# Two Winograd pairs per feed-forward column group, with the weight sums prepared in HBM by accumulating transfers

## The chip, the cores and the metric

The kernel runs on one core of one Trainium2 chip. A time is the device time of one execution in microseconds (us); the number to compare is the median over runs. A core has five engines with instruction queues of their own: TensorE (PE, matrix products), VectorE (DVE), ScalarE (ACT), GpSimd (POOL) and SyncE (SP). SP and POOL issue most of this kernel's DMA transfers. Each queue is worked off in order, so an instruction that waits holds back everything behind it on the same queue.

## The reference, cut to what matters

One decoder layer on 256 tokens of width 2048, all in float32: an input projection, two kinds of token mixers, an output projection, a gated feed-forward layer with a causal width-3 convolution, and a last gated addition. The change concerns the feed-forward layer:

```python
h = rms_norm(x, ffn_norm_g[i])
u = h @ w_up[i]                       # (256, 2048) @ (2048, 2 * 5632)
a, g = jnp.split(u, 2, axis=-1)       # two halves of 5632 columns
a = causal_dwconv(a, conv_w[i], conv_b[i])
x = x + (jax.nn.gelu(a, approximate=False) * g) @ w_down[i]
```

## The kernel before, in words

**Products.** Every weight block that PE uses is first split into two float32r parts, `hi` (a cast on ACT) and `lo` (raw minus `hi`, on DVE). A product of a 128 x 128 block of activations (kept as hi and lo too) with a 128 x 512 block of weights is then three matmuls: hi·hi, hi·lo and lo·hi. The function `three` (line 1291) issues them for the up projection.

**The stages.** First stretch: input projection, mixers and output projection run as 153 weight blocks of up to 512 KB, streamed by `run_stream` with three raw buffers, three blocks split ahead of PE. Then the feed-forward layer and the last gate run as a list of units handled by `run_units`: a unit has a load (SP), a split (ACT and DVE, four pairs of `hi`/`lo` buffers) and a function that issues matmuls. The up projection is 11 column groups `q` of 4 x 128 columns of `a` and the matching 512 columns of `g`. Tokens come in two halves t = 0, 1 and the columns in two halves n = 0 (`a`) and n = 1 (`g`), so a group has four PSUM banks. A plain unit takes one chunk `k` of 128 inputs: 4 products, 12 matmuls.

**The seven.** In groups 1 to 10 the chunks k = 0 and 1 are not plain. With the chunks and token halves as a 2 x 2 block matrix on the left, and chunks and column halves as one on the right, Winograd's scheme makes the same result with seven products in place of eight: 21 matmuls for 24. Three products (P5, P6, P7) use sums of left blocks `S_up` (made once by `up_sums`), and sums of right blocks, that is, of weights. The kernel before makes these weight sums on DVE in every group: `seven` loads four blocks into `xs` (line 1314 to 1316), three subtractions (lines 1323 to 1325) make T1, T2 and T4, and four units split and multiply. P1, P5, P6, P7 go to four banks of their own; lines 1355 to 1361 combine them into `z_up` (in `xs`), scaled, which is added to the group's rows later.

**The end of a group.** `up_rows` (ACT, line 887) scales the four banks into `EZ`; `up_turn` adds `z_up` (DVE, line 894), transposes 32 x 32 blocks into `Y` (DVE, line 184) and `move` (line 186) issues 16 DMA transfers from `Y` back to `EZ`, all on POOL. In the next group the jobs of `up_act` follow, spread over units: `first` copies the `a` half into `Y` (ACT, line 901), four `conv` jobs make the convolution into `c_`, the second half of `Y` (ACT line 906, DVE line 909), and `last` does GELU, the product with `g`, and the split (lines 915, 916, 140, 141). The left sums of the down projection go to HBM (`sums<-Sp`, POOL).

**What sets the order.** Python code issues the instructions; a scheduler of the framework then places them on each queue by its own estimate of times. `tc.issue_after(...)` keeps an instruction behind a given one. Raw buffers in the up projection are the three of `raw` and five spare ones (`v0` to `v4`); `free_raws` says which unit may use which.

Of the kernel before, what the change touches and what calls it, by code (L numbers as in the profile page):

```python
# [9 lines left out]
F32 = mybir.dt.float32  # L10
# [35 lines left out]
LOAD_AT, SUMS_AT, SEVEN_AT = 5, 2, 6  # L46
# [3 lines left out]
def layer_kernel(  # L50
# [135 lines left out]
    def move(y, c):  # L186

        for a in range(4):
            for b in range(4):
                pool.dma_start(out=c[32 * b : 32 * b + 32, a::4], in_=y[32 * a : 32 * a + 32, :, b])  # L190
# [54 lines left out]
    def run_stream(blocks, pulls, ramp=False):  # L245
# [4 lines left out]
        for i in range(-AHEAD_DMA, nb):  # L250
            j = i + AHEAD_DMA
            if j < nb:
# [5 lines left out]
                nc.sync.dma_start(out=raws[j][:, : kb * n].rearrange("p (k n) -> p k n", k=kb), in_=src)  # L258

# [17 lines left out]
            if i >= 0:  # L277
                blocks[i][1](*parts.pop(i))
                done[0] += 1
                pull(pulls)  # L280

# [3 lines left out]
    def token_group(w, korder, actT, c0, n, finish, tag="mm", prep=None, load=None):  # L285
# [26 lines left out]
        return blocks  # L312

# [29 lines left out]
    with mixers:  # L343
# [462 lines left out]
        run_stream(blocks, 2, ramp=True)  # L806
# [3 lines left out]
    with tc.tile_pool(name="ffn", bufs=1) as fp:  # L810
# [6 lines left out]
        S_up = fp.tile([P, 4, 256], F32R, tag="u42", name="S_up")  # L817
        spares = {"u32": (4, 2), "u36": (4, 2), "u40": (2, 1)}
        spare_raws = {k: fp.tile([P, n // 2, BLK], F32, tag=k, name=f"{k}r") for k, (n, _) in spares.items()}
# [26 lines left out]
        B_up = xs[:, 0]  # L846
# [11 lines left out]
        def sums_of(u, f, t):  # L858

            (a11, a21), (a12, a22) = ((u[:, j, 0:P], u[:, j, P:S]) for j in range(2))  # L860
            dve.tensor_add(f[:, 0], a21, a22)
            dve.tensor_sub(f[:, 1], f[:, 0], a11)
            dve.tensor_sub(f[:, 2], a11, a21)
            dve.tensor_sub(f[:, 3], a12, f[:, 1])
# [12 lines left out]
        c_ = Y[:, BLK : 2 * BLK].rearrange("p (k s) -> p k s", k=4)  # L877
# [11 lines left out]
        def up_turn(q):  # L889
# [6 lines left out]
            move(y, Z)  # L896

        def up_act(q):

# [32 lines left out]
        def free_raws(j):  # L932

            def may(t):
                if t[0] == "v":
                    return 7 <= j < 16 + 18 * until[t]
# [4 lines left out]
        def new_raw(j, name):  # L941
# [7 lines left out]
            if tag[0] == "v":  # L949
                i = int(tag[1])  # L950
                return spare_raws[f"u{32 + 4 * (i // 2)}"][:, i % 2]
# [48 lines left out]
        def part(hi, lo, raw):  # L1000
            act.copy(hi, raw)  # L1001
            last["hi"] = traced()
            dve.tensor_sub(lo, raw, f32(hi))  # L1003
# [30 lines left out]
        def down(c0, X_tag, P_tag, sums_done, done, at, pairs, sevens):  # L1034
# [39 lines left out]
            def seven(p_, hook):  # L1074
# [24 lines left out]
                def split3(hi, lo):  # L1099
                    ra, rb_ = first.raws  # L1100
                    dve.tensor_sub(half(ra, 0), half(ra, 1), half(ra, 0))
                    dve.tensor_sub(half(ra, 1), half(rb_, 1), half(ra, 1))  # L1102
# [6 lines left out]
                def split4(hi, lo):  # L1109
                    ra, rb_ = first.raws  # L1110
                    dve.tensor_sub(half(rb_, 1), half(rb_, 1), half(ra, 0))
                    dve.tensor_sub(half(rb_, 0), half(rb_, 0), half(rb_, 1))
# [28 lines left out]
        def sums_done(c0):  # L1141

            def f(b):
                both = xs[:, 1, c0 : c0 + 1024].rearrange("p (n c) -> p n c", n=2)
                x00, x01 = (xs[:, 0, c0 + n * 512 : c0 + (n + 1) * 512] for n in range(2))
                right = xs[:, :, c0 + 512 : c0 + 1024]

                def twice(v):
# [310 lines left out]
```

## Time and profile before

| | us |
|---|---|
| median of 3 runs | 1241.52 |
| lowest and highest run | 1240.97, 1242.49 |
| the profiled execution, its own time | 1241.07 |
| its span in the profile | 1239.1 |

The span is the time from the first to the last recorded instruction. Of the up projection, group 0 begins near 444 us and group 10 ends near 918 us; the down projection and the gate follow. The busy time of an engine is not by itself a cost: what counts is where PE waits. "Landing" is the time from a transfer's issue to its completion.

### The profile page before, as it was taken

The page shows a single profiled execution, that of the slowest core. Times are in us where ns is not written, and L with a number is a line of the kernel's source. Part 1 is how long each engine was busy: PE and PEld are TensorE (multiplying, and loading weights), DVE is VectorE, ACT ScalarE, POOL GpSimd, SP SyncE. Part 2 cuts the span into 40 slices and gives each one's busy share as a digit, 9 for nine tenths or more (in the row PEclk, how much of TensorE's full clock was granted, in tenths as well). Part 3 has the DMA queues.
Part 4 walks back from the last instruction along what each step waited for, and adds up shares of the span by engine and source line. Part 5 has one row for each costly group of instructions (what it writes and reads, how often), then busy time and mean ns, then how long its engine had stood idle before and what let it go on. Part 6 is the DMA issues. An engine that isn't in the chain of part 4 may idle for free.

```text
span 1239.1 us, 16191 instructions
## 1 busy us (share of the span) xinstructions
PE 1232.5 (99%) x5638; PEld 1039.3 (84%) x5638; DVE 901.0 (73%) x1125; ACT 720.9 (58%) x1000; POOL 244.2 (20%) x457
## 2 busy tenths in 40 slices
PE   9999999999999999999999999999999999999998
PEld 7999988888888888888888888888888888888887
DVE  5455566665565665888888898888778998998653
ACT  7565455554554454766676576657645555566542
POOL 2001256513304202022202211220220000050000
PEclk9999999999999999999999999999999999999999
DMA  8766877766557797776877777676895996777560
GB/s 242 207 187 185 233 215 220 207 194 177 173 187 223 217 340 219 223 227 217 260 236 212 224 254 243 192 237 193 257 294 171 316 359 204 264 236 251 179 211 34
DMA packets 134370, 276.35 MB, mean 223 GB/s; under 512 B 15065, under 2 KB 30033, under 8 KB 134161
## 3 DMA queue, kind: packets, MB, share of 16 engines
q1 hardware_dynamic: 118864, 249.66, 64.3%
q0 software_dynamic: 15040, 25.50, 7.2%
q8 instruction: 44, 0.72, 0.2%
q14 instruction: 37, 0.30, 0.1%
q10 hardware_dynamic: 385, 0.16, 0.0%
HBM read 247.46 MB, written 8.93 MB: 207 GB/s over the span
## 4 chain that ended last, share of the span: by engine, by line
PE 99%; DMA 0%; SPq 0%; DVE 0%; ACT 0%; issue 0%; DVEq 0%
PE tg L304 13%; PE tg L305 13%; PE tg L306 13%; PE up L1292 12%; PE up L1294 12%; PE up L1293 12%; PE dnP L1054 1%; PE dnP L1055 1%; PE dnP L1053 1%; PE upP L1292 1%; PE upP L1294 1%; PE upP L1293 1%; PE dn(0, 1)_7885 L1055 1%; PE dn(0, 0)_7881 L1054 1%; PE dn(0, 1)_7885 L1054 1%; PE dn(1, 0)_7889 L1054 1%
## 5 line engine op out<-in xcount | busy, mean ns | idle before, releaser
L275 DVE TENSOR_TENSOR lo<-raw,hi 128x1024 fp32r<-128x1024 f32 (+3 forms) x153 | 177.7, 1162 | 154.8 <-ACT hi L273 154.4
L1294 PE MATMUL up<-hi,x2T 128*128 128x512 f32 x644 | 250.7, 389 | 0.0
L1293 PE MATMUL up<-lo,x2T 128*128 128x512 f32 x644 | 250.6, 389 | 0.0
L273 ACT CAST hi<-raw 128x1024 fp32r<-128x1024 f32 (+3 forms) x153 | 153.1, 1001 | 155.3 <-PE tg L306 122.7
L1292 PE MATMUL up<-hi,x2T 128*128 128x512 f32 x644 | 221.3, 389 | 0.0
L305 PE MATMUL tg<-lo,hT 128*128 128x512 f32 (+2 forms) x480 | 181.5, 379 | 0.0
L304 PE MATMUL tg<-hi,hT 128*128 128x512 f32 (+2 forms) x480 | 180.9, 382 | 0.0
L306 PE MATMUL tg<-hi,hT 128*128 128x512 f32 (+2 forms) x480 | 180.3, 377 | 0.0
L1003 DVE TENSOR_TENSOR lo<-raw,hi 128x1024 fp32r<-128x1024 f32 (+1 forms) x118 | 137.2, 1171 | 43.4 <-ACT hi L1001 42.8
L1001 ACT CAST hi<-raw 128x1024 fp32r<-128x1024 f32 (+1 forms) x118 | 118.8, 1014 | 81.6 <-PE up L1294 35.9
L1294 PEld LDWEIGHTS up<-hi,x2T 128*128 128x128 f32 x644 | 120.9, 188 | 25.1
L1293 PEld LDWEIGHTS up<-lo,x2T 128*128 128x128 f32 x644 | 120.9, 188 | 25.0
L1292 PEld LDWEIGHTS up<-hi,x2T 128*128 128x128 f32 x644 | 120.9, 188 | 25.0
L190 POOL DMA_DIRECT2D EZ<-Y x176 | 93.1, 536 | 122.7 <-DVE Y L184 52.1
L306 PEld LDWEIGHTS tg<-hi,hT 128*128 128x128 f32 x480 | 90.1, 188 | 12.5
L305 PEld LDWEIGHTS tg<-lo,hT 128*128 128x128 f32 x480 | 90.2, 188 | 11.7 <-DVE lo L275 0.3
L304 PEld LDWEIGHTS tg<-hi,hT 128*128 128x128 f32 x480 | 89.7, 188 | 11.7
L1001 ACT CAST hi<-xs 128x1024 fp32r<-128x1024 f32 (+1 forms) x43 | 40.8, 952 | 71.1 <-PE up L1294 50.0
L1003 DVE TENSOR_TENSOR lo<-xs,hi 128x1024 fp32r<-128x1024 f32 (+1 forms) x43 | 47.1, 1098 | 34.7 <-ACT hi L1001 34.7
L873 POOL DMA_DIRECT2D sums<-Sp x9 | 5.2, 575 | 272.3 <-DVE Sp L866 272.3
L1003 DVE TENSOR_TENSOR lo<-u36r,hi 128x1024 fp32r<-128x1024 f32 x36 | 43.6, 1215 | 11.8 <-ACT hi L1001 10.3
L1001 ACT CAST w<-raw 128x1024 fp32r<-128x1024 f32 x27 | 28.4, 1053 | 38.3 <-DVE raw L1102 27.1
(695 smaller groups left out, 2351.9 us busy)
## 6 DMA issues: line engine op xcount, KB each, us to landing
raw<-in_w_in_dram SPq DMA_DIRECT2D x71, 512.0 KB, 4.2
raw<-in_w_up_dram SPq DMA_DIRECT2D x68, 512.0 KB, 5.2
raw<-in_w_down_dram SPq DMA_DIRECT2D x43, 512.0 KB, 6.0
u36r<-in_w_up_dram SPq DMA_DIRECT2D x36, 512.0 KB, 5.0
raw<-in_w_in_dram SPq DMA_DIRECT2D x40, 432.0 KB, 3.8
raw<-in_w_out_dram SPq DMA_DIRECT2D x32, 512.0 KB, 4.7
u32r<-in_w_up_dram SPq DMA_DIRECT2D x31, 512.0 KB, 5.2
EZ<-Y POOLq DMA_DIRECT2D x176, 64.0 KB, 4.6
```

Source lines behind the costliest of these rows:

```text
L190: pool.dma_start(out=c[32 * b : 32 * b + 32, a::4], in_=y[32 * a : 32 * a + 32, :, b])
L273: act.copy(hi, raw[:, :w])
L275: dve.tensor_sub(lo, raw[:, :w], f32(hi))
L304: pe.matmul(o, ah, hi[:, i, :], start=first, stop=False)
L305: pe.matmul(o, ah, lo[:, i, :], start=False, stop=False)
L306: pe.matmul(o, al, hi[:, i, :], start=False, stop=last)
L1001: act.copy(hi, raw)
L1003: dve.tensor_sub(lo, raw, f32(hi))
L1054: pe.matmul(o, ah, lo, start=False, stop=False)
L1292: pe.matmul(o, ah, hi, start=start, stop=False)
L1293: pe.matmul(o, ah, lo, start=False, stop=False)
L1294: pe.matmul(o, al, hi, start=False, stop=stop)
```

## The change

**Two sevens per group.** In groups 1 to 10 the chunks k = 0 to 3 are taken by two sevens (`SEVENS_UP` = 2); 12 plain units are left instead of 14. P1, P5, P6 and P7 of the two are summed in the same four banks, so that the combination of line 1355 to 1361 is still made once. A group has 20 units: four plain, the first seven's four, three plain, the second seven's four, five plain (`FIRST_AT`, `SECOND_AT`).

**The weight sums come from HBM.** `up_jobs` makes for each of the 20 sevens a DRAM tile `upT` of four 128 x 512 slots: a plain transfer on SP copies a block into two slots, accumulating transfers on POOL add blocks to them (two in the first job), a second SP transfer copies slot 0 to slots 2 and 3, and three more accumulating transfers add to these. Signs in `sums_of`, `sums_done` and the down projection's splits are turned so that only additions are needed. Twelve of the 20 sets are made during the first stretch (from block 18 on, every 11 blocks, the second job 12 blocks after the first), the other eight during groups 0 to 5 (from unit 12 on, every 14 units, the second job 7 units later). A seven's units then load like weights: 512 KB, 512 KB, 512 KB and 256 KB. The subtractions of lines 1323 to 1325 and the `B_up` loads are gone.

**Conv results in memory of their own.** `c_` is now in `xs` (except in the last group), not in `Y`; the spare raw buffer `v4` is in `xs` too. The jobs of `up_act` sit at units 9, 10, 11, 12, 15 and 16 of a group's 20 (before: 10 to 15 of 18). `move` puts every other transfer on SP, eight on each queue. The `lo` subtraction that follows an `up_turn` is kept behind it.

POOL's queue before, at the end of the first stretch and the first up groups (`x2z` is the residual's transposed rows, `EZ<-Y` the moves of a group's end, `sums<-Sp` the left sums):

```order
L190 DMA x2z<-x2y 32x2x128 x48
L165 TENSOR_TENSOR rstd_ffn<-rs_v,neghalf 128x2
L190 DMA EZ<-Y 32x2x256 x32
L873 DMA sums<-Sp 128x1024
L190 DMA EZ<-Y 32x2x256 x16
```

and the same place now (L332 is an accumulating transfer; the moves are L193):

```order
L168 TENSOR_TENSOR rstd_ffn<-rs_v,neghalf 128x2
L332 DMA upT_1_158<-in_w_up_dram 128x512
L332 DMA upT_0_159<-in_w_up_dram 128x512 x2
L193 DMA EZ<-Y 32x2x256 x8
L332 DMA upT_0_159<-in_w_up_dram 128x512 x3
L332 DMA upT_1_160<-in_w_up_dram 128x512 x4
L193 DMA EZ<-Y 32x2x256 x7
L332 DMA upT_1_160<-in_w_up_dram 128x512
L193 DMA EZ<-Y 32x2x256
L332 DMA upT_0_161<-in_w_up_dram 128x512 x5
```

Eight moves of a group now stand behind accumulating transfers, which themselves wait for copies or for each other; in group 1 one move stands behind the last of them.

SP's queue before, around the loads of a seven in the up projection (L986 loads a unit, L1314 to L1316 load the seven's blocks):

```order
L986 DMA raw_0_4253<-in_w_up_dram 128x2x512
L1314 DMA xs<-in_w_up_dram 128x2x512
L1315 DMA xs<-in_w_up_dram 128x512
L1316 DMA xs<-in_w_up_dram 128x512
L986 DMA u32r<-in_w_up_dram 128x2x512 x2
```

and now, around the end of group 0 (L1018 loads a unit, L329 is a plain copy into `upT`):

```order
L329 DMA upT_0_159<-in_w_up_dram 128x2x512
L1018 DMA u36r<-in_w_up_dram 128x512
L1018 DMA u36r<-in_w_up_dram 128x2x512
L1018 DMA raw_0_4436<-in_w_up_dram 128x2x512
L193 DMA EZ<-Y 32x2x256 x8
L1018 DMA raw_0_4476<-upT_1_148 128x1024
L1018 DMA raw_0_4498<-upT_1_148 128x1024
L1018 DMA u32r<-in_w_up_dram 128x2x512
L1018 DMA u32r<-in_w_up_dram 128x512
L329 DMA upT_0_159<-upT_0_159 128x2x512
```

The loads now share SP with the copies and with half of the moves, and the second copy of a set waits for an accumulating transfer.

The diff, cut to its core:

```diff
-LOAD_AT, SUMS_AT, SEVEN_AT = 5, 2, 6
+SEVENS_UP, FIRST_AT, SECOND_AT = 2, 4, 7
+CONV_AT = (9, 10, 11, 12, 15, 16)
+U_FROM, U_STEP, U_GAP = 18, 11, 12
+UP_EARLY = 12
...
-                pool.dma_start(out=c[32 * b : 32 * b + 32, a::4], in_=y[32 * a : 32 * a + 32, :, b])
+                (other if other and b % 2 else pool).dma_start(out=c[32 * b : 32 * b + 32, a::4], in_=y[32 * a : 32 * a + 32, :, b])
...
+    def up_jobs(q, r):
+
+        w = w_up[0, 2 * r * P : (2 * r + 2) * P].rearrange("(a p) (h c) -> a h p c", p=P, h=2)[:, :, :, q * 512 : (q + 1) * 512]
+        t = up_T[q, r] = kp.tile([P, 4, 512], F32, name=f"upT{q}_{r}")
+
+        def copied(i, src):
+            with tc.issue_after(last["load"]):
+                nc.sync.dma_start(out=t[:, i : i + 2], in_=src.unsqueeze(1).broadcast_to([P, 2, 512]))
+
+        def added(i, src):
+            pool.dma_start(out=t[:, i], in_=src, accum_op=ALU.add)
+        return (lambda: (copied(0, w[0, 1]), added(0, w[0, 0]), added(1, w[1, 1])),
+                lambda: (copied(2, t[:, 0]), added(2, w[1, 1]), added(3, w[1, 1]), added(3, w[1, 0])))
...
-        run_stream(blocks, 2, ramp=True)
+        jobs = {}
+        all_T = [up_jobs(q, r) for q in range(1, KF // 4) for r in range(SEVENS_UP)]
+        for i, fs in enumerate(all_T[:UP_EARLY]):
+            for j, f in enumerate(fs):
+                jobs.setdefault(U_FROM + U_STEP * i + U_GAP * j, []).append(f)
+        assert max(jobs) < len(blocks)
+        run_stream(blocks, 2, ramp=True, jobs=jobs)
...
-        c_ = Y[:, BLK : 2 * BLK].rearrange("p (k s) -> p k s", k=4)
+        c_own = [v.rearrange("p (k s) -> p k s", k=4) for v in (xs[:, 0, 0:BLK], Y[:, BLK : 2 * BLK])]
...
-            move(y, Z)
+            last["turned"] = traced()
+            with tc.issue_after(last["load"]):
+                move(y, Z, nc.sync)
...
-            dve.tensor_sub(lo, raw, f32(hi))
+            with ExitStack() as st:
+                if "turned" in last:
+                    st.enter_context(tc.issue_after(last.pop("turned")))
+                dve.tensor_sub(lo, raw, f32(hi))
...
-                sums = (lambda: dve.tensor_sub(T[:, 0:BLK], B[:, 512 : 512 + BLK], B[:, 0:BLK]),
-                        lambda: dve.tensor_sub(half(T, 2), b22, half(T, 0)),
-                        lambda: dve.tensor_sub(half(T, 3), b21, half(T, 2)))
...
+                def fn1(hi, lo):
+                    sum_of(5, S(1), hi[:, 0], lo[:, 0])
+                    sum_of(7, S(3), hi[:, 1], lo[:, 1])
+
+                def fn2(hi, lo):
+                    sum_of(6, S(2), hi[:, 0], lo[:, 0])
+                    three(st["b"][1, 0], *left(2 * r + 1, 1), hi[:, 1], lo[:, 1])
+
+                def fn3(hi, lo):
+                    three(st["b"][0, 0], *left(2 * r + 1, 0), hi[:, 0], lo[:, 0])
+                    three(st["b"][0, 1], *S(4), hi[:, 1], lo[:, 1])
+
+                def fn4(hi, lo):
+                    sum_of(1, left(2 * r, 0), hi[:, 0], lo[:, 0])
...
+                return [Unit([t[:, 0:2]], fn1), Unit([t[:, 2:4]], fn2), Unit([w[2 * r + 1, :, :, c]], fn3),
+                        Unit([w[2 * r, :, 0:1, c]], fn4)]
...
-            return us[:SEVEN_AT] + se + us[SEVEN_AT:], load
+            return us[:FIRST_AT] + seven(0) + us[FIRST_AT:SECOND_AT] + seven(1) + us[SECOND_AT:]
...
+        for i, fs in enumerate(all_T[UP_EARLY:]):
+            for j, f in enumerate(fs):
+                with_after(us[12 + 14 * i + 7 * j], between(f))
...
-                    with_after(plains[q + 1][i], between(job))
+                    with_after(plains[q + 1][CONV_AT[i]], between(job))
```

121 lines of the change are left out of this document (48 added, 73 removed).

## The prediction, on record before the changed kernel was run

> **What bounds the kernel now.** I read the page's busy times first, then PE's waits, then the chain that ended last, the stretches by time, and last the single groups of the up projection. The page (share of the span, instructions):
>
> ```profile
> span 1239.1 us, 16191 instructions
> PE 1232.5 (99%) x5638; PEld 1039.3 (84%) x5638; DVE 901.0 (73%) x1125; ACT 720.9 (58%) x1000; POOL 244.2 (20%) x457
> ```
>
> A busy PE alone proves little, so its waits (waited for: us in all, times, longest):
>
> ```profile
> PE warm L93 <- DVE ones L89: 1.1, 1, 1.1
> PE xT L152 <- DMA xs<-in_x_dram: 1.0, 1, 1.0
> ```
>
> These are all, and both lie at the start. From there PE issues without a gap: its matmuls are the time, and only fewer or faster ones can shorten it. The price of one comes from the chain that ended last (start us, us, what):
>
> ```profile
> 496.41 0.91 PE up L1292 x4
> ...
> 539.25 0.91 PE up L1292 x4
> ```
>
> The same place of two neighbouring groups: 42.84 us for 14 plain units of 12 matmuls and a seven of 21, 189 in all, so 0.2267 us each. A plain unit is then 2.72 us.
>
> The transfers and the other engines in stretches (us, busy times, PEclk, DMA share, GB/s):
>
> ```profile
> 442.00:456.00 14.00, 14.00 (x64) 11.58 (x63) 7.35 (x7) 6.52 (x7) 0.00 (x0) 1.00 1.05 391
> 486.00:490.00 4.00, 4.00 (x19) 3.30 (x19) 2.10 (x4) 1.05 (x1) 2.81 (x6) 1.00 1.08 299
> 60.00:444.00 384.00, 384.00 (x1811) 331.31 (x1810) 231.48 (x348) 207.75 (x355) 118.73 (x214) 1.00 0.70 206
> 618.00:661.00 43.00, 43.00 (x191) 35.63 (x190) 36.71 (x44) 28.21 (x33) 9.05 (x17) 1.00 0.76 232
> ```
>
> After PE, DVE (third pair) is busy 36.71 of 43 us in an up group, ACT 28.21. Transfers run at 232 GB/s there and 206 in the first stretch; the most that plain loads are seen to hold is 391, at a share of 1.05, and 299 at 1.08 with moves beside them. The clock is 1.00 throughout.
>
> **The change part by part.**
>
> *Matmuls.* Ten groups replace two plain units (24) by a second seven (21): 30 fewer, 30 x 0.2267 = **6.80 us**, all on the path.
>
> *DVE and ACT in a group* (mean ns of one behind the busy time):
>
> ```profile
> L1003 DVE TENSOR_TENSOR lo<-u36r,hi 128x1024 fp32r<-128x1024 f32 x32 | 38.7, 1214 | 5.9 <-ACT hi L1001 5.9
> L1001 ACT CAST hi<-u36r 128x1024 fp32r<-128x1024 f32 x32 | 33.5, 1052 | 15.6 <-PE up L1294 14.8 <-DVE lo L1003 0.8
> L1323 DVE TENSOR_TENSOR xs<-xs 128x1024 f32<-128x1024 f32 x9 | 11.0, 1217 | 0.0
> L1325 DVE TENSOR_TENSOR xs<-xs 128x512 f32<-128x512 f32 x10 | 6.8, 684 | 0.0
> ```
>
> Splits go from 17 full and one half to 18 full and two halves, about 1.5 full ones more: DVE +1.90 us, ACT +1.6. The three subtractions leave DVE: 1.22 + 2 x 0.68 = 2.58. DVE comes to 36.0, ACT to 29.8 of a group's 42.84 - 0.68 = 42.16 us. Cost nothing, covered by PE; if bunching broke that cover, PE would wait. The tightest place is a group's end (timeline; POOL's `EZ<-Y` are the moves):
>
> ```profile
> 648.19 2.36 DVE L894 TENSOR_TENSOR EZ<-EZ,xs 128x1024 f32<-128x1024 f32 x2 [0.16 <-ACT EZ L887]
> 650.47 1.24 DVE L184 STREAM_TRANSPOSE Y<-EZ 128x1024 f32<-128x1024 f32 x1
> ...
> 653.33 1.24 DVE L184 STREAM_TRANSPOSE Y<-EZ 128x1024 f32<-128x1024 f32 x1
> ...
> 654.87 3.71 POOL L190 DMA_DIRECT2D EZ<-Y  x7 [0.58 <-DVE Y L184]
> ...
> 664.21 0.39 PE L1292 MATMUL upP<-hi,x2T 128*128 128x512 f32 x1
> ...
> 665.33 1.58 POOL L190 DMA_DIRECT2D EZ<-Y  x3 [1.76 <-DMA EZ<-Y]
> ...
> 674.93 1.03 ACT L901 COPY Y<-EZ 128x1024 f32<-128x1024 f32 x1
> ```
>
> The seven starts at 664.21, six plain units into the group, which so begins at 664.21 - 16.32 = 647.89. The turn now stays in one piece on DVE: adds to +2.6 us, two transposes of 1.16 to +4.9, then the split for the fourth unit, done at +6.1. PE reaches that unit at 3 x 2.72 = 8.16: 2 us to spare.
>
> *Moves, and who waits for them.* Before, the last of 16 moves leaves POOL at 666.9 (+19.0), and `first` starts at 674.93 (+27.0). Now eight moves on each queue, at 0.53 us a piece from +5.1, leave by +9.4. `first` comes behind the cast of unit 13, whose buffer is free when PE ends unit 9: 4 x 2.72 + 21 x 0.2267 + 2 x 2.72 = +21.1, so +22.1 with the cast. Queued behind `first` on ACT is the cast of unit 14, which PE wants at 21.1 + 2.72 + 18 x 0.2267 = +27.9; taking 1.0 + 0.6 + 0.6 of ACT and 0.7 of DVE off, `first` may start as late as +25.0. Landing times (KB each, median us):
>
> ```profile
> raw<-in_w_in_dram SPq DMA_DIRECT2D x71, 512.0 KB, 4.2
> ...
> u32r<-in_w_up_dram SPq DMA_DIRECT2D x31, 512.0 KB, 5.2
> EZ<-Y POOLq DMA_DIRECT2D x176, 64.0 KB, 4.6
> ...
> kept_x<-xs SPq DMA_DIRECT2D x1, 2048.0 KB, 9.3
> ```
>
> With 4.6 us the moves are in at +14.0: 11 us are left for whatever POOL waits for ahead of them. That wait is new: an accumulating transfer waits for its copy to land. No row shows a transfer from HBM to HBM or an accumulating one; by the nearest rows one landing is 4.6 us (64 KB) to 9.3 (2 MB), and a 256 or 512 KB one belongs near the 5.2 of a 512 KB load. One such wait, even of 9.3, fits. I take nothing.
>
> *Issue time.* POOL loses 88 moves and gets 100 accumulations, +6 us; SP gets 88 moves and 40 copies, at the same 0.53 some 70 us over 1239, on a queue that mostly waits for buffers. Behind SP's new waits (a turn, a set's second copy) stand unit loads, and they have this much room (timeline):
>
> ```profile
> 669.66 2.27 SPq L986 DMA_DIRECT2D u32r<-in_w_up_dram  x2
> ...
> 685.49 1.06 ACT L1001 CAST hi<-u32r 128x1024 fp32r<-128x1024 f32 x1 [0.71 <-PE up L1294]
> ```
>
> Issued 15.8 us before the cast, landed in 5.2: 10 us free. A second copy comes 7 units after the first, so its condition is normally long met. Nothing.
>
> *Bytes.* A seven pair loads 1792 KB in place of 1024: +1.57 MB a group. A set moves two copies of 512 KB and five additions of 256 KB, 2.36 MB. In the first stretch a set each 11 blocks of 2.9 us (153 blocks in 444 us) adds 74 GB/s to 206: 280, far under 391. In groups 0 to 5 eight sets in 105 units are 1.52 a group: 232 GB/s x 43 us = 9.98 MB, + 1.57 + 3.6 = 15.1 MB in 42.16 us, 359 GB/s, 92% of 391. By shares it is tighter: 0.76 x 43 = 32.7 us of all 16 engines, plus 5.2 MB at 391, 13.2: 45.9, which at the highest share seen, 1.08, takes 42.5 us, 0.3 over a group. Shares swell when queues are thin, so I go by the rate: covered, nothing. A gain is excluded, since PE has no wait to give back in these stages. The upper end is the first rival.
>
> *Rest.* The turned signs swap adds for subtractions of the same shapes. `c_` out of `Y` removes a wait of DVE, none of PE's.
>
> The sum: 1241.07 - 6.80 = 1234.3 for the profiled execution; the median stands 0.45 above it, so **1234.7**. Small waits at single group ends would bring it up to 1236.5.
>
> **The rivals.**
>
> *Additions read twice, and the transfers become the bound in groups 0 to 5* (slower). An accumulating transfer must also read its target. If that doubles the price of its bytes, 1.52 x 1.31 = 2.0 MB more a group. By rate: 17.1 MB / 391 = 43.9 us, 1.7 over, for 5.25 groups 9 us: 1244. By share: 45.9 + 5.1 = 51.0, over 1.08 47.2 us, 5.1 over: 27 us, 1262. It turns the result round once a group costs 1.3 us more than its 42.16. For it: 92% before any doubling. Against: units have 10 us of lead, and the sets wait for each other, two or three transfers in flight at most. The Trainium skill, "Collectives: The Full Stack", section "The bandwidth ceiling: the fold count and why AG ≠ RS ≠ AR", says that an adding transfer is slower than a copying one not for the adding but because it reads two sources, about half the rate; by that the 1244 to 1262 just worked out would hold, by the 391 row alone 1234.7. No row of before can decide it.
>
> *POOL's queue makes the moves late* (gain partly eaten, at worst all). Two waits in a row ahead of a group's moves, 2 x 9.3 = 18.6 us against 11, hold ACT and then PE 7.6 us; at 5.2 each nothing happens. The order of group 1 and group 5 has such rows. One turn: 1242.3; a turn that is late by 2 or 3 us: 1237.
>
> *The first stretch runs short of raw buffers* (slower).
>
> ```profile
> 231.21 1.23 DVE L275 TENSOR_TENSOR lo<-raw,hi 128x1024 fp32r<-128x1024 f32 x1 [0.16 <-ACT hi L273]
> ...
> 232.46 11.95 SPq L258 DMA_DIRECT2D raw<-in_w_in_dram  x5
> ...
> 239.00 1.05 ACT L273 CAST hi<-raw 128x1024 fp32r<-128x1024 f32 x1 [0.20 <-ACT PT L571]
> ```
>
> A freed buffer is loaded at 232.46 and cast at 239.00: 6.5 us, of which landing takes 4.2. Only a lasting 2.3 us more would bound the stage, a third of the excess per block: 1 us over, for the 130 blocks with sets, is 43 us, 1278. Against: sets move for at most 2.36 MB / 391 = 6 of each 32 us, and PE is three blocks behind the splits.
>
> **How the numbers follow.** The forecast 0.57; the transfers as bound 0.18; late moves 0.17 (0.10 of it still faster, the rest about even or slower); the first stretch 0.08. Within 0.2% (2.5 us, about what this kernel's runs can tell) is little: 0.08. Faster 0.67, slower 0.25. The forecast's own range is 1234.0 to 1236.5. The range to be held 8 times in 10 goes from 1233.8 (no stage has more to give than the 6.8, and the runs scatter by 0.75) to 1252, the middle of the first rival; what is beyond is half of that rival and the third, under 0.2.
>
> **What would show it.** Right: PE without waits after the start, a group at 42.16 us, DVE near 36 and ACT near 30 in it, landing of unit loads still near 5 us. Wrong by the first rival: DMA share at 1.05 or more through groups 1 to 5 and `raw` waits on DMA there, gone from group 6 on. Wrong by the second: ACT's line-901 copies waiting for `EZ<-Y`, POOL idle on `upT` ahead of the moves. Wrong by the third: `hi` waiting for `raw` between 60 and 444 us. Wrong altogether if an accumulating transfer lands in more than some 10 us: then both queues block.

## The result and the profile after

The changed kernel takes **1340.11 us** (median of 4 runs, 1338.47 to 1343.76) against 1241.24 (1240.65 to 1242.49) of the kernel before on the same chip: 1.0799 times as long, 95% interval 1.0774 to 1.0825. The forecast was 1234.7; the time lies 105.4 us above it and outside the range. The profiled execution took 1338.92.

The page of the changed kernel (span; PE's busy time, share and instructions; the two large DMA queues with packets, MB and share of 16 engines' span; q0 is the queue that POOL issues to, q1 SP's):

```profile
span 1337.2 us, 16517 instructions
PE 1268.2 (95%) x5608; PEld 1047.1 (78%) x5608; DVE 898.2 (67%) x1123; ACT 738.0 (55%) x1023; POOL 284.1 (21%) x469
q1 hardware_dynamic: 139824, 292.14, 66.8%
q0 software_dynamic: 26624, 45.95, 17.4%
```

The 30 matmuls are gone (5638 before, 5608 now), so the gain that was summed is there, and it is drowned. PE sits idle for 1337.2 - 1268.2 = 69.0 us, where it was 6.6. And it is busy for 35.7 us longer with 30 matmuls fewer, so it is also slower where it is busy. PE's waits, the longest groups (us in all, times, longest):

```profile
PE tg L311 <- DVE lo L279: 10.4, 14, 3.3
PE up L1322 <- ACT hi L1033: 10.2, 6, 3.3
PE upP L1322 <- ACT hi L1033: 8.8, 6, 2.4
PE sc L571 <- ACT qk L554: 7.2, 1, 7.2
```

PE waits for splits, everywhere: `tg` is the first stretch, `up` and `upP` the up projection. ACT's waits, one step further back:

```profile
ACT hi L277 <- DMA raw<-in_w_in_dram: 127.9, 68, 5.0
ACT hi L277 <- DMA raw<-in_w_out_dram: 34.5, 20, 4.8
ACT hi L1033 <- DMA raw<-in_w_up_dram: 30.4, 15, 7.4
ACT hi L1033 <- DMA raw<-upT: 23.3, 8, 6.9
ACT qk L554 <- DMA keptM<-M: 11.3, 1, 11.3
```

The casts wait for weights; before, such waits for `in_w_in` were 14.8 us in all. The stretches (us, busy times of PE, PEld, DVE, ACT, POOL, then PEclk, DMA share, GB/s):

```profile
60.00:484.00 424.00, 390.53 (x1757) 328.31 (x1756) 216.96 (x325) 198.27 (x338) 165.21 (x267) 0.97 0.89 238
...
613.00:656.00 43.00, 40.58 (x170) 32.59 (x169) 33.19 (x37) 26.13 (x31) 9.01 (x14) 0.96 1.02 297
656.00:699.00 43.00, 41.10 (x172) 33.10 (x171) 31.86 (x38) 24.50 (x30) 10.02 (x16) 0.96 0.99 297
```

The landing times (KB each, median us):

```profile
raw<-in_w_up_dram SPq DMA_DIRECT2D x72, 512.0 KB, 9.0
raw<-in_w_in_dram SPq DMA_DIRECT2D x71, 512.0 KB, 6.4
upT<-in_w_up_dram POOLq DMA_DIRECT2D x100, 256.0 KB, 8.2
```

The DMA share adds up the times of a stretch's packets, so that packets which overlap can take it past 1. It is 0.89 in the first stretch (0.70 before) and 0.99 to 1.02 in the up groups (0.76), while the bytes per second are only 238 and 297, far from the 391 that the row of 442 to 456 us had held. Loads of 512 KB land in 6.4 us in place of 4.2, and in 9.0 in the up projection. Where the time went, by the first matmul of the up projection, before and after:

```profile
432.10 0.39 PE L1292 MATMUL up<-hi,x2T 128*128 128x512 f32 x1
```

```profile
483.66 0.39 PE L1322 MATMUL up<-hi,x2T 128*128 128x512 f32 x1
```

The first stretch lost 51.6 us. The up projection went from 432.1 to 904.7 (its first and last matmul before; the 444 and 918 given further up are some 12 us late), 472.6 us, to 483.7 to 996.2, 512.5 us, where 472.6 - 6.8 = 465.8 had been due: 46.7 lost. The rest, 334.4 us before and 341.0 after, lost 6.6. Together 104.9.

The timeline also gives each group its time, from its first matmul to the next group's. In the run without the sets (below) group 0 takes 44.4 us and groups 1 to 8 take 42.2 each, as forecast. In the changed kernel group 0 takes 55.6, groups 1 and 2 take 42.2 and 43.2, groups 3 to 6 take 46.7 to 49.4, groups 7 to 9 take 42.2 to 43.2, and group 10 takes 51.3. So the loss of the up projection has three places: group 0, right behind the first stretch (11.2 us), groups 2 to 6, where sets are still being made (25), and the last two groups (some 10).

**The slower busy time.** At the longest wait, where PE stands from 194.2 to 201.4 us, the granted clock falls. The timeline, then windows of 1 us, then the clock over the span:

```profile
201.40 0.80 PE L571 MATMUL sc<-qk 128*128 128x128 f32 x2 [7.18 <-ACT qk L554]
```

```profile
197.00:198.00 1.00, 0.00 (x0) 0.00 (x0) 0.00 (x0) 0.00 (x0) 0.00 (x0) 0.50 0.55 163
...
205.00:206.00 1.00, 1.00 (x4) 0.81 (x3) 0.01 (x1) 0.00 (x0) 0.36 (x2) 0.50 0.55 178
...
207.00:208.00 1.00, 1.00 (x6) 0.82 (x5) 0.36 (x2) 0.16 (x1) 0.10 (x1) 1.00 0.86 330
```

```profile
core 0: 1337.2 us, clock 0.978
```

From 196.5 to 206.7 the clock is 0.50, so for some 5 us after PE has its work again its matmuls run at half speed. Much shorter waits are followed by half speed too (a wait of 1.37 us, and a window behind it):

```profile
799.00 0.50 PE L1322 MATMUL up<-hi,x2T 128*128 128x512 f32 x1 [1.37 <-ACT hi L1033]
```

```profile
801.00:802.00 1.00, 1.00 (x4) 0.81 (x3) 0.63 (x1) 1.00 (x2) 0.00 (x0) 0.50 1.11 340
```

Over the span the clock is 0.978 where it was 1.00, which is at most 0.022 x 1337 = 29 us of matmul time. Before the last microsecond of the span it is 0.50 in 13 stretches, 58.0 us together: ten of 3.4 us, two of 6.8 and one of 10.2. PE has no work in 7.5 of them, so the clock costs some 50 / 2 = 25 us. The Trainium skill, "TensorE: Matmul & The Clock Gate", section "Part 1: The HAM clock gate (the "warmup" mystery)", says that the clock is halved after an idle window of about 3.4 us and comes back after as long a busy one. The trace agrees with the length of these windows, but not with so long an idle time as the condition: ahead of seven of the 13 stretches the longest wait is only 1.4 to 2.5 us, and in the wait of 7.2 us the clock is halved after 2.3 us.

### The profile page after: what moved, and what is told of

It reads as the page before. It is cut to its first block, busy times and chain, and to the rows that moved or that the text cites. A ratio compares the mean times of both kernels' runs of the same rounds, so it can differ in the third digit from the quotient of the medians.

```text
span 1337.2 us, 16517 instructions
## 1 busy us (share of the span) xinstructions
PE 1268.2 (95%) x5608; PEld 1047.1 (78%) x5608; DVE 898.2 (67%) x1123; ACT 738.0 (55%) x1023; POOL 284.1 (21%) x469
## 3 DMA queue, kind: packets, MB, share of 16 engines
q0 software_dynamic: 26624, 45.95, 17.4%
## 4 chain that ended last, share of the span: by engine, by line
PE 50%; DMA 29%; DVE 8%; ACT 6%; issue 4%; SPq 2%; POOL 1%; ACTq 0%; DVEq 0%; POOLq 0%
DMA raw<-in_w_in_dram 9%; PE up L1323 5%; PE up L1324 5%; PE up L1322 5%; PE tg L311 4%; PE tg L312 4%; PE tg L310 4%; DMA upT<-in_w_up_dram 3%; DMA raw<-in_w_up_dram 2%; DMA upT<-upT 2%; DVE lo L279 2%; ACT hi L277 2%; DVE lo L1038 2%; DMA raw<-in_w_out_dram 2%; ACT hi L1033 2%
## 5 line engine op out<-in xcount | busy, mean ns | idle before, releaser
L1324 PE MATMUL up<-hi,x2T 128*128 128x512 f32 x584 | 231.9, 397 | 0.0
L1038 DVE TENSOR_TENSOR lo<-raw,hi 128x1024 fp32r<-128x1024 f32 (+1 forms) x150 | 169.9, 1141 | 82.9 <-ACT hi L1033 80.1
L1033 ACT CAST hi<-raw 128x1024 fp32r<-128x1024 f32 (+1 forms) x150 | 146.9, 987 | 128.9 <-PE up L1324 35.8
L1322 PE MATMUL up<-hi,x2T 128*128 128x512 f32 x584 | 179.8, 397 | 10.3 <-ACT hi L1033 10.2
L332 POOL DMA_DIRECT2D upT<-in_w_up_dram x100 | 85.0, 1003 | 348.8 <-DMA upT<-in_w_up_dram 245.8
L1322 PEld LDWEIGHTS up<-hi,x2T 128*128 128x128 f32 x584 | 111.4, 192 | 36.3 <-ACT hi L1033 13.2
L1324 PEld LDWEIGHTS up<-hi,x2T 128*128 128x128 f32 x584 | 111.8, 191 | 22.9
L1038 DVE TENSOR_TENSOR lo<-u36r,hi 128x1024 fp32r<-128x1024 f32 (+1 forms) x49 | 57.5, 1173 | 33.7 <-ACT hi L1033 33.2
L1033 ACT CAST hi<-u36r 128x1024 fp32r<-128x1024 f32 (+1 forms) x49 | 49.7, 1014 | 51.3 <-DMA u36r<-upT 18.5
L193 POOL DMA_DIRECT2D EZ<-Y x88 | 48.5, 609 | 65.3 <-ACT hi L1033 24.7
L1038 DVE TENSOR_TENSOR lo<-u32r,hi 128x1024 fp32r<-128x1024 f32 (+1 forms) x42 | 48.5, 1170 | 12.4 <-ACT hi L1033 11.9
L310 PE MATMUL tg<-hi,catT 128*128 128x512 f32 x128 | 50.4, 395 | 3.9 <-ACT catT L204 3.3
```

Of the source, the lines that this page charges most:

```text
L193: (other if other and b % 2 else pool).dma_start(out=c[32 * b : 32 * b + 32, a::4], in_=y[32 * a : 32 * a + 32, :, b])
L310: pe.matmul(o, ah, hi[:, i, :], start=first, stop=False)
L332: pool.dma_start(out=t[:, i], in_=src, accum_op=ALU.add)
L1322: pe.matmul(o, ah, hi, start=start, stop=False)
L1324: pe.matmul(o, al, hi, start=False, stop=stop)
```

## The experiments

Theories, formed on the trace of the changed kernel: (A) the sets, that is the transfers that make the weight sums in HBM, take the loss, and in them the double read of an accumulating transfer; (B) the three raw buffers of the first stretch turn longer landings into waits; (C) POOL's queue makes moves late; (D) the order of units and buffers in the up projection loses time of itself, with no set in sight.

### Without the sets

```diff
-        all_T = [up_jobs(q, r) for q in range(1, KF // 4) for r in range(SEVENS_UP)]
+        all_T = []
...
-                return [Unit([t[:, 0:2]], fn1), Unit([t[:, 2:4]], fn2), Unit([w[2 * r + 1, :, :, c]], fn3),
+                return [Unit([w[2 * r, :, :, c]], fn1), Unit([w[2 * r, :, :, c]], fn2), Unit([w[2 * r + 1, :, :, c]], fn3),
```

> No sets are made: the two sevens of a group load plain weight blocks of the same number in place of the weight sums (so the feed-forward result is not the reference's), all else as in the changed kernel. If the sets' transfers cause the whole loss: 1234.7 us, between 1233.5 and 1238, PE without waits, a group of 42.16 us. If the schedule of two sevens, the moves on two queues or the new places of the conv jobs cost PE time: above 1245, with waits of PE at fixed units of each group.

Measured: **1246.24 us** (1244.93 to 1246.85), ratio 1.0037 (1.0023 to 1.0051). So 93.9 of the 105.4 us are the sets' (A), and 11.5 are not (D); the time lies in the second range, above 1245. Where the 11.5 lie (windows, then a wait of ACT, then a row of the page that is wanted below):

```profile
60.00:432.00 372.00, 372.00 (x1754) 321.30 (x1753) 221.13 (x328) 199.41 (x338) 118.03 (x213) 1.00 0.70 202
432.00:930.00 498.00, 491.39 (x2155) 403.78 (x2154) 401.89 (x466) 331.49 (x393) 52.41 (x98) 1.00 0.81 267
870.00:880.00 10.00, 6.42 (x20) 4.39 (x19) 3.14 (x3) 2.96 (x4) 0.00 (x0) 0.83 0.82 259
```

```profile
ACT hi L1032 <- DMA raw<-in_w_up_dram: 18.8, 13, 6.9
```

```profile
q0 software_dynamic: 12224, 19.73, 5.5%
```

The first stretch is as before. PE's gaps are at 830 to 920 us, in the last up groups, where the spare raw buffers `v0` to `v3` have been given back. At the longest gap something else stands in the way as well (SP's queue, then the cast of ACT that waits):

```profile
864.03 6.23 SPq L193 DMA_DIRECT2D EZ<-Y  x8
870.37 1.90 SPq L1017 DMA_DIRECT2D raw<-in_w_up_dram  x3
```

```profile
873.36 0.62 ACT L1032 CAST hi<-raw 128x512 fp32r<-128x512 f32 x1 [6.92 <-DMA raw<-in_w_up_dram]
```

SP issued its last load before these at 857.3, stood until 864.0 for the turn whose results it moves, and took 6.2 us to issue the eight moves. Only then could the late load leave, although the split of a raw buffer, which frees it, had ended at 865.1. So the half of the moves on SP's queue has a part in the 11.5 us, beside the buffers. No run takes the moves off SP with all else left as it is, so the two are not told apart.

### The spares kept longer

The same kernel without sets, with a longer lease of those buffers:

```diff
-                    return (24 if t == "v4" else 7) <= j < 16 + (16 + 2 * SEVENS_UP) * (until[t] - 1) + (6 if t == "v4" else 16)
+                    return (24 if t == "v4" else 7) <= j < 16 + (16 + 2 * SEVENS_UP) * (until[t] - 1) + (6 if t == "v4" else 32)
```

> The kernel without the sets (the sevens load plain blocks in their place, as in the first run here, so that the output is not the reference's), but with the four spare raw buffers v0 to v3 kept for 16 units longer at the end of the up stage. The run without the sets took 1246.24, and all that it lost lies at 830 to 920 us of the span, where ACT waits 18.8 us for raw w_up blocks. Theory (the last up groups run short of raw buffers, since a seven's unit of 512 KB feeds the matmuls for less time than a plain one): with the longer lease the run takes 1234.5 to 1238, the sum of the prediction. Rival (the loss is of another kind, say casts or gelu work that come late): it stays at 1244 to 1248.

Measured: **1239.97** (1238.48 to 1243.39, 10 runs), ratio 0.9993 (0.9983 to 1.0003). The lease was 6.3 of the 11.5 us; the theory held in kind, though the median stayed 2 us above its range. What is left shows in PE's waits:

```profile
PE up L1321 <- ACT hi L1032: 2.1, 1, 2.1
PE dn(0, 0)_7963 L1088 <- DVE w L1037: 2.0, 1, 2.0
```

4.1 us more of waits than before: the profiled execution took 1238.62, and without them it would be at 1234.5, next to the prediction's sum of 1234.3. So 30 x 0.2267 was right. The wait of 2.1 us stands at the same turn as the longest gap above, again behind eight moves on SP (862.0 to 867.8). But even with its sums for nothing, and the longer lease, the second seven made no measurable gain.

### Early and late sets alone

Only the 12 sets of the first stretch (`UP_EARLY`), and only the eight of groups 0 to 5; a seven without its set loads plain blocks.

```diff
-        all_T = [up_jobs(q, r) for q in range(1, KF // 4) for r in range(SEVENS_UP)]
+        all_T = [up_jobs(q, r) for q in range(1, KF // 4) for r in range(SEVENS_UP) if 2 * (q - 1) + r < UP_EARLY]
```

> Only the twelve early sets are made; the sevens of groups 7 to 10 load plain blocks in place of sums (result not the reference's there). If the two stages lose apart: the first up matmul starts near 484 us as in the changed kernel (432 before) and the up stage takes about 42.2 us a group, 1285 to 1295 in all. If the late sets alone are to blame: 1240.

```diff
-        all_T = [up_jobs(q, r) for q in range(1, KF // 4) for r in range(SEVENS_UP)]
-        for i, fs in enumerate(all_T[:UP_EARLY]):
+        all_T = [None] * UP_EARLY + [up_jobs(q, r) for q in range(1, KF // 4) for r in range(SEVENS_UP) if 2 * (q - 1) + r >= UP_EARLY]
+        for i, fs in enumerate([]):
```

> Only the eight late sets are made, in groups 0 to 5; the sevens of groups 1 to 6 load plain blocks in place of sums (result not the reference's there). If the two stages lose apart: the first up matmul starts near 432 us, groups 1 to 5 are slower by 5 to 9 us each, 1275 to 1290 in all. If the loss in the up stage comes from what the first stretch left behind: 1240.

Measured: early alone **1317.64** (1317.11 to 1318.17), 71.4 us above the kernel without sets; late alone **1272.44** (1271.88 to 1273.01), 26.2 above it. 1246.2 + 71.4 + 26.2 = 1343.8 against 1340.1 measured with both: the two are nearly additive. Both missed their ranges, the early one by 23 us above, the late one by 3 below; the first up matmul of the early one is at 487.5 us. The windows of the early and of the late one:

```profile
60.00:432.00 372.00, 335.80 (x1520) 283.12 (x1519) 187.02 (x291) 173.62 (x304) 139.31 (x223) 0.96 0.89 234
```

```profile
60.00:432.00 372.00, 372.00 (x1755) 321.26 (x1754) 221.24 (x328) 199.26 (x339) 118.01 (x213) 1.00 0.70 202
432.00:930.00 498.00, 480.23 (x2064) 388.99 (x2063) 383.25 (x448) 318.49 (x379) 81.87 (x129) 0.98 0.92 290
```

Each kind loses time where its transfers run, and the early ones in group 0 too: it takes 54.9 us with the early sets alone and 44.4 with the late ones alone.

### Plain copies in place of accumulating transfers

Same bytes written, same issues and waits, no adding:

```diff
-            pool.dma_start(out=t[:, i], in_=src, accum_op=ALU.add)
+            pool.dma_start(out=t[:, i], in_=src)
```

> The 100 accumulating transfers become plain copies of the same blocks to the same slots, on the same queue, in the same order and with the same waits (so the slots hold blocks, not sums). If the price of an accumulating packet is the cause (2 KB at about 177 ns against 84 in the two traces): the adds' 142 us of all 16 engines become 67, and the time falls to 1250 to 1280. If the waits that the sets put into POOL's and SP's queues are the cause, these stay, and the time stays above 1315. If any extra transfers of this size are too many: 1290 to 1320.

Measured: **1289.04** (1288.32 to 1289.75): 51.1 us of the changed kernel's loss come from the adding alone. The time falls between two of the ranges, 9 us above the first theory's. Its queue:

```profile
span 1288.0 us, 16517 instructions
q0 software_dynamic: 20224, 45.95, 11.5%
```

q0's time is its share of the span: 0.174 x 1337.2 = 232.7 us of all 16 engines in the changed kernel, 0.115 x 1288.0 = 148.1 here, 0.055 x 1243.4 = 68.4 without sets. The same 45.95 - 19.73 = 26.2 MB take 164.3 us when added and 79.7 when copied: **2.06 times as long**, 160 against 329 GB/s. The packet counts differ as well: less the 12224 of the run without sets, the additions went in 14400 packets and the copies in 8000. That is not what doubles the time: in the packet records of the changed kernel a plain packet of 2 KB takes 84 ns in the median and one of 4 KB 159, while those of 2 KB on POOL's queue, four fifths of them additions, take 176. The Trainium skill, "Collectives: The Full Stack", section "The bandwidth ceiling: the fold count and why AG ≠ RS ≠ AR", says of collectives that a reduce-scatter runs at about half the rate of an all-gather, because each addition needs two source reads; the 2.06 of these transfers, on a single core, agrees with that half. That the second read is the cause is the page's reason; the runs show the factor.

### A fourth raw buffer in the first stretch

The changed kernel, all of it, with one buffer more for the 153 blocks (the attention's `PT` pays with one of its two):

```diff
-                raws[j] = wp.tile([P, BLK], F32, tag="raw", name=f"raw{j}", bufs=RAW)
+                raws[j] = mp.tile([P, BLK], F32, tag="raw4", name=f"raw{j}", bufs=1) if j % 4 == 3 else wp.tile([P, BLK], F32, tag="raw", name=f"raw{j}", bufs=RAW)
...
-                    PT = mp.tile([P, 384], F32, tag="PT", name="PT", bufs=2)
+                    PT = mp.tile([P, 384], F32, tag="PT", name="PT", bufs=1)
```

> The changed kernel with a fourth raw buffer in the first stretch alone (every fourth block's weights land in it; the attention's PT tile gives up one of its two buffers to make room). Everything is computed. In the changed kernel the first up matmul starts at 483.7 us of the span instead of 432.1, and the cast of ACT waits 127.9 us for its raw blocks (68 waits) where it waited 14.8. Theory, the landing time (three buffers go round in issue, 6.4 us of landing, cast, and 6.4 us over three buffers is more than one block's time): with four buffers a landing of 6.4 us is covered, most of the 51.6 us comes back, the first up matmul starts at 435 to 450 and the run takes 1290 to 1306. Rival, the bandwidth (the added bytes and the sums' double reads fill the transfers while the sets are made, however many buffers there are): the first up matmul stays at 475 or later and the run takes 1328 or more. In between would mean that both have a part.

Measured: **1311.06** (1308.08 to 1314.03), 29.0 us less than the changed kernel. It is the case in between: theory (B) has a part, and so has the bandwidth. The timeline's first matmul of the up projection, the first stretch, and PE's longest wait:

```profile
461.86 0.39 PE L1322 MATMUL up<-hi,x2T 128*128 128x512 f32 x1
```

```profile
60.00:462.00 402.00, 380.68 (x1765) 326.35 (x1764) 217.87 (x327) 200.97 (x340) 165.03 (x267) 0.98 0.93 252
```

```profile
PE sc L571 <- ACT qk L554: 9.9, 1, 9.9
```

21.8 of the 51.6 us came back, the share rose to 0.93, and the longest wait, 9.9 us, is now one of the attention.

### The fourth buffer and plain copies

> The run with a fourth raw buffer, with the adding transfers made plain copies (the sets then hold no sums, so the output is not the reference's; same bytes moved, same issues, same waits). Without the fourth buffer this edit took the changed kernel from 1340.1 to 1289.0 and its first up matmul from 483.7 to 453.2. Theory (the double read of an adding transfer is what takes landing times past what the buffers cover, in the first stretch and behind it): the first up matmul starts at 434 to 444 and the run takes 1268 to 1282. Rival (with four buffers the adds' price is covered, and the remaining loss is the number of transfers): 1295 or more.

Measured: **1262.89** (1262.49 to 1263.28), better than either theory had it. The same two rows of it:

```profile
435.12 0.39 PE L1322 MATMUL up<-hi,x2T 128*128 128x512 f32 x1
```

```profile
60.00:435.00 375.00, 373.58 (x1756) 321.23 (x1755) 220.96 (x328) 200.57 (x341) 149.08 (x270) 1.00 0.89 269
```

The first stretch is nearly whole: 435.1 for 432.1, though loads of 512 KB still land in 5.8 us there. With the two runs before, the four cases make a square:

| | accumulating | plain copies | difference |
|---|---|---|---|
| three buffers | 1340.1 | 1289.0 | 51.1 |
| four buffers | 1311.1 | 1262.9 | 48.2 |
| difference | 29.0 | 26.1 | |

The adding costs about 50 us with either number of buffers, and the missing buffer 26 to 29 with either kind of transfer.

### The control for the fourth buffer

> The control for the fourth buffer: the kernel without sets and with the longer lease of the spares (1239.97 us; its sevens load plain blocks, so that the output is not the reference's), with the fourth raw buffer of the first stretch and one PT buffer instead of two. If neither matters where transfers land in time: 1238.5 to 1241.5, first up matmul at 431 to 434. If the second PT buffer was needed: 1243 or more.

Measured: **1241.74** (1238.93 to 1243.55, 10 runs), ratio 1.0001 (0.9992 to 1.0011), a hair above the first range and below the second; the first up matmul starts at 433.42. The edit itself neither costs nor gives anything that these runs can tell: the same kernel with three buffers had 0.9993 (0.9983 to 1.0003).

### The early sets in more pieces

For theory (C), on top of the fourth buffer: `up_jobs` gives five pieces some blocks apart, so that an accumulating transfer comes longer after the one that it depends on:

```diff
+        return two, ((0, lambda: copied(0, w[0, 1])), (3, lambda: (added(0, w[0, 0]), added(1, w[1, 1]))), (8, lambda: copied(2, t[:, 0])),
+                     (11, lambda: (added(2, w[1, 1]), added(3, w[1, 1]))), (14, lambda: added(3, w[1, 0])))
...
-            for j, f in enumerate(fs):
-                jobs.setdefault(U_FROM + U_STEP * i + U_GAP * j, []).append(f)
+            for at, f in fs[1]:
+                jobs.setdefault(min(U_FROM + U_STEP * i + at, len(blocks) - 1), []).append(f)
```

> The run with a fourth raw buffer (1311.06 us, first up matmul at 461.9 us, longest PE wait 9.9 us: sc for ACT's qk, behind keptF and keptM, which landed 13.0 and 12.6 us after their issue on POOL's queue instead of 3.4), with the early sets issued in five pieces some blocks apart instead of two, so that POOL never reaches an adding transfer whose destination is still in flight, and its small moves aren't queued behind such a wait (POOL waits 148.0 us for transfers to upT in 0 to 490 us there). Bytes, adds and buffers are the same. Theory (part of the first stretch's loss is POOL's queue, with the small moves of the attention late behind the adds): the wait of 9.9 us goes, the first up matmul starts at 446 to 454 and the run takes 1297 to 1305. Rival (only the transfers' own time counts): the first up matmul stays at 458 to 466 and the run takes 1307 to 1315.

Measured: **1313.93** (1312.93 to 1314.93): no gain, and the first up matmul comes at 470.5 us, later than either range. But the edit did not take POOL's waits away, as the theory asks. From 0 to 490 us POOL waits 168.7 us for transfers to `upT` (94.9 for additions, 73.8 for second copies), where it had waited 155.5 (148.0 and 7.5). So this run shows that moving these waits does not help, and leaves open what they cost. The wait of PE that it was to remove is still there (PE's wait, and the landing of the small transfer behind it):

```profile
PE sc L573 <- ACT qk L556: 9.8, 1, 9.8
```

```profile
keptF<-aFT POOLq DMA_DIRECT2D x1, 12.0 KB, 11.2
```

`keptF` is 12 KB, and landed in 3.4 us before the change, in 12.4 after it (13.0 with four buffers), and with plain copies in 6.2 (8.1 with four buffers). It is issued without a wait of its own, right behind two transfers of 256 KB on the same queue, here behind three. Between 140 and 212 us of this run, `rowF` transfers of 128 KB on the same queue landed in 3.5 us. This points to the packets that stand ahead of `keptF` in its queue as the reason; it is not shown, since no run has the attention's moves on another queue.

### Versions with the sums in SBUF

Could the second seven pay, with its sums made by other means? Each pair is loaded once, and an engine adds in `xs`, from where the splits read (everything is computed; the longer lease of the spares is kept):

```diff
+                def make():
+                    if pair or not hasattr(first_, "raws"):
+                        return
+                    pair["made"] = True
+                    en = {"pool": pool, "dve": dve}[eng]
+                    b1, b0 = (v.rearrange("p (h c) -> p h c", h=2) for v in first_.raws)
+                    for o, x, y in ((0, b0[:, 1], b0[:, 0]), (1, b0[:, 1], b1[:, 1]), (2, T[:, 0], b1[:, 1]), (3, T[:, 2], b1[:, 0])):
+                        en.tensor_tensor(out=T[:, o], in0=x, in1=y, op=ALU.add)
```

Both sevens' sums on POOL:

> A version without any sums in HBM: a seven loads its two chunks of weights once, as a pair of raw buffers, and POOL makes the four sums of a pair in SBUF, from where ACT and DVE split them as they do raw blocks. Same matmuls as in the changed kernel, 24 x 1.5 MB fewer loads of sums, no adding transfers, spares v0 to v3 kept longer as in the run beside it. If the matmul count is what is left when the sets are gone: 1234.5 to 1238. If the sums on POOL come late (POOL also makes the transfers that turn the groups' rows): a wait of ACT for POOL shows in each of groups 1 to 6, 1 to 3 us each, 1241 to 1253.

The first seven's on DVE, the second's on POOL:

> The same with the sums of the first seven of a group on DVE and those of the second on POOL. DVE is busy 36.0 us of a group of 42.16 as changed, the conv among it; four sums of 128 x 512 more would be some 2 to 3 us. If POOL's sums are the late ones this is better than the version with both on POOL (half the waits, 1236 to 1244); if DVE is the tighter engine it is worse (1240 to 1250).

Both on POOL, asked for earlier and further apart, with all moves on POOL:

```diff
-SEVENS_UP, FIRST_AT, SECOND_AT = 2, 4, 7
+SEVENS_UP, FIRST_AT, SECOND_AT = 2, 4, 9
...
-SUM_ON, HOOK_AT = ("pool", "pool"), (2, 7)
+SUM_ON, HOOK_AT = ("pool", "pool"), (1, 6)
...
-                move(y, Z, nc.sync)
+                move(y, Z)
```

> The version with the four sums of each pair made by POOL in SBUF (1298.46 us: in a group of some 42 us the casts waited for POOL's sums, and those for their loads, which stood on SP's queue behind the half of the moves that SP issues), with all moves back on POOL's queue, the two sevens five plain blocks apart instead of three, and the sums asked for earlier (behind the casts of unit 1 and of unit 6 of a group). If the late loads and sums were the loss: 1236 to 1248, with waits of ACT for POOL's sums under 15 us in all. If POOL (sums of 1.3 to 2.2 us and 16 moves a group) or the buffers held by pairs are too slow as such: 1265 to 1300.

Measured: **1298.46** (1297.32 to 1299.70), **1293.19** (1292.49 to 1294.33) and **1294.69** (1294.34 to 1295.11). All ranges missed but the worst one of the third. In the second version (ACT's wait; then POOL's and DVE's additions, busy us, mean ns):

```profile
ACT hi L1033 <- POOL xs L1396: 81.5, 20, 7.7
```

```profile
L1396 POOL TENSOR_TENSOR xs<-xs,u32r 128x512 f32<-128x512 f32 x12 | 20.6, 1720 | 0.5
L1396 DVE TENSOR_TENSOR xs<-xs,u32r 128x512 f32<-128x512 f32 x12 | 8.3, 689 | 0.0
```

An addition takes POOL 1.7 us and DVE 0.69, and what the casts wait for is POOL. The third version took that wait down to 15.7 us, and others came in its place (PE's and ACT's):

```profile
PE up L1324 <- DVE lo L1038: 22.5, 9, 3.2
...
ACT Y L931 <- DMA EZ<-Y: 31.1, 8, 6.1
```

Eight additions more a group on DVE would be 8 x 0.69 = 5.5 us on top of the 36.0 that the prediction found for a group of 42.16. That would leave 0.7 us free, and no run tried it. No version here that computes the layer beats the kernel before.

## Why the prediction was wrong

*Matmuls: right.* 5608 are issued, and without the sets and with the longer lease the profiled time less its 4.1 us of new waits is 1234.5.

*Bytes: the step that failed.* The prediction had two ways to price the sets, and chose: "Shares swell when queues are thin, so I go by the rate: covered, nothing." The way not chosen would have been near for groups 0 to 5, but only with the additions at twice the price, as the first rival had them; without the doubling it gave 0.3 us over a group. A set takes 164.3 / 20 = 8.2 us of all 16 engines for its additions, and 0.668 x 1337.2 - 0.686 x 1243.4 = 40.2 us over 20, 2.0, for its copies: 10.2 us, where 2.36 MB at 391 GB/s had been 6.0.

- First stretch: 0.70 x 372 = 260 us of all engines were already taken, 12 sets add 122, and 382 of 372 us is no longer "far under". A rate in bytes hid this, since 206 GB/s of small and large transfers together held the engines for 0.70 of the time, while 391 GB/s at 1.05 had been large loads alone. With plain copies a set comes to (79.7 + 40.2) / 20 = 6.0, 12 of them to 72, the share to 332 / 372 = 0.89, as the row of the run with four buffers and plain copies has it.
- Groups 0 to 5: eight sets are 82 us in 5.25 x 42.16 = 221. Without sets the share of the up projection is 0.81, so up to the 1.02 of the row at 613 us there is room for 0.21 x 221 = 46 and up to the 1.08 of before for 60: 22 to 36 us over. Measured, 26.2.

*The first rival, additions read twice: its price was right*, twice a copy's for 2.06 measured, and 0.18 too little; that the second read is the reason, no run shows. Its "5.1 over: 27 us, 1262" for groups 0 to 5 stands against the 26.2 measured, and 25 of the changed kernel's loss lie in groups 2 to 6. It was confined to these groups; the first stretch, where the same price falls on three buffers, was left to another rival without the doubling.

*The third rival, raw buffers in the first stretch: right as well*, at 0.08. It said that 2.3 us more of landing would bound the stage, and for "1 us over" 43 us. The median landing rose by 2.2, to 6.4, so that the blocks beside sets are past that point and the others are not, and the stretch lost 51.6. "Against: sets move for at most 2.36 MB / 391 = 6 of each 32 us" was the mistake: 10.2, and transfers that share the engines make each other's landing longer, not only their own sum.

*Issue time and loads: "Nothing" was wrong by 11.5 us*, in the last groups, where 15.8 us of lead had been read from a row of group 5, with all spares in use. 6.3 of it is the spares' lease; a seven's unit of 512 KB is used up by two products, not four, so that the same buffers cover less time. The step also found 10 us of room for loads that stand behind a turn on SP. At the longest gap SP was held for 12.4 us, 6.2 of waiting and 6.2 of issuing: a move takes SP 0.78 us there, not the 0.53 that POOL needs. The remaining 5.2 are the 4.1 us of waits and the scatter of the medians.

*Moves and the second rival, POOL's queue: mostly not so.* At the group ends POOL waits 8.7 us in all for transfers to `upT` ahead of moves, in seven waits of at most 2.3, and ACT's first copies do not wait for the moves. One wait that belongs to POOL's queue arose elsewhere, 7.2 us behind `keptF` and `keptM` in the first stretch. What stands ahead of them in the queue is the likely reason, and that is not shown.

*What no step had:* a stall is paid for twice. PE's idle time rose by 62.4 us, and the other 42.5 of the 104.9 us are busy time at a slower pace, of which the stretches at half clock explain some 25. Another 8 are idle time that is counted as busy: a matmul's record lasts 0.39 us where the next one starts after 0.23, so that each of PE's 52 waits hides about 0.16. The remaining 9 or so are not settled.

*The order of the costs*, from the runs, from the forecast's 1234.7: the new schedule without any sets 11.5, to 1246.2; the sets as plain transfers, with four buffers, 16.7, to 1262.9; the adding 48.2, to 1311.1; the missing fourth buffer 29.0, to 1340.1.

## What to carry to other kernels

Price added transfers in the time that they hold the DMA engines (share times span), not in bytes per second, against the share already taken in that very stretch; and read an accumulating transfer at twice the time of a copy until a run says otherwise. Where a stream has few buffers, ask what its landing time becomes beside the new transfers, and divide by the number of buffers: a stage can be lost long before the share reaches 1. A matmul engine that is made to wait can also work more slowly afterwards (here at half clock for 3.4 us or more, after waits from 1.4 us up), so a stall can cost more than its length. And moving transfers to another queue puts them ahead of what that queue already carries: ask how long the queue then stands, and what waits behind it.

## What the runs showed of the hardware that had not been expected

- The same 26.2 MB from HBM to HBM took 164.3 us of all engines as accumulating transfers and 79.7 as copies (2 KB packets of 176 ns against 84); a 256 KB accumulating transfer landed in 8.2 us beside the other work, a copy in its place in 6.4.
- A 12 KB transfer right behind two or three accumulating ones of 256 KB on the same queue landed in 11.2 to 13.0 us instead of 3.4; behind two plain ones in 6.2 and 8.1.
- After a wait of 7.2 us the clock stood at 0.50 for 10 us, 5 of them with PE at work again; after a wait of 1.4 us it stood at 0.50 for 3.4.
- SP took 6.2 us to issue eight moves of 64 KB, 0.78 each, where POOL had taken 0.53 each.
- POOL adds two 128x512 blocks in 1.3 to 2.3 us in nearly all cases, DVE in 0.69.
